# A hybrid encoder trunk: two projections moved up one place in the recurrent mixer, the last gates placed inside the output projection's first group, low parts issued ahead of recurrence steps

## The chip, the cores and the metric

The kernel runs on one core of a Trainium2 chip. The metric is the device time of one execution in microseconds, as a median of runs. A core has five engines that work side by side, each through its own instructions in order: PE (matmul), DVE (vector), ACT (scalar and lookup functions), POOL (general purpose) and SP (here it issues most DMAs). PE's weight loads are shown apart as PEld and overlap its matmuls.

## The reference, cut to what matters

Two layers over 1024 frames of width 1024, in float32. Layer 0 is a recurrent mixer and an MLP, layer 1 is chunked attention and an MLP. The change lies in layer 0's mixer and in the norms in front of the two MLPs.

```python
def recurrent_mixer(hn, w_in, conv_w, conv_b, gate_a_w, gate_a_b, gate_x_w, gate_x_b, lam, w_out):
    z = hn @ w_in
    gate, xr = jnp.split(z, 2, axis=-1)
    xr = causal_depthwise_conv(xr, conv_w, conv_b)
    y = rg_lru(xr, gate_a_w, gate_a_b, gate_x_w, gate_x_b, lam)
    return (y * jax.nn.gelu(gate)) @ w_out

def rg_lru(x, w_a, b_a, w_x, b_x, lam):
    ...
    r = jax.nn.sigmoid(jnp.einsum("bsnd,nde->bsne", xb, w_a).reshape(bsz, s, w) + b_a)
    i = jax.nn.sigmoid(jnp.einsum("bsnd,nde->bsne", xb, w_x).reshape(bsz, s, w) + b_x)
    log_a = (-LRU_C * r.astype(jnp.float32)) * jax.nn.softplus(-lam.astype(jnp.float32))
    a = jnp.exp(log_a)
    mult = jnp.sqrt(-jnp.expm1(2.0 * log_a))
    u = mult * (i * x).astype(jnp.float32)
    ...
    _, h = lax.associative_scan(combine, (a, u), axis=1)
```

The recurrence width is 1408: 11 tiles of 128 channels for the projections and the convolution, and 16 blocks of 88 channels for the gate weights. After the mixer comes `h = h + g1 * y`, then the second norm and a squared-ReLU MLP.

## The kernel before

**Arithmetic.** Everything lies transposed, channels on partitions and the 1024 frames in two halves of 512. Each float32 operand is split in a high part (a cast on ACT, line 196 for streamed data) and a low part (source minus high part, on DVE, line 200). A product is three matmuls of 512 columns: high by high, high by low, low by high (`mm3`, lines 329, 330 and 331).

**The stream.** Class `Stream` holds a list of items in the order in which they are loaded: weights, gate weights, modulation rows ("ada", used by one DVE operation at line 362 each), and rows of intermediate results that were put in DRAM. At most seven raw items lie in the chip at once; a later one is loaded by SP only when an earlier one is given back. Queue "w" turns weights into parts, queue "a" operands; `cap` bounds how many parts of each may be live. The casts are issued as soon as the caps allow; the low parts are put on a list (`los`) and are issued by `flush`.

**The tick.** The program order of the mixer is written out by hand. A call of `tick` stands after every few matmuls. It runs the jobs that are due (`at(d, f)` puts a job d ticks later: convolution copies, scans, products), then issues low parts up to a cost (`flush`; 2 in the mixer, where a low part of 512 columns costs 1 and one of 1024 costs 2), and then pumps the stream, which loads and casts. What is issued earlier stands earlier in each engine's queue.

**The mixer's steps.** `xr(t)` is the projection of channel tile t: 48 matmuls, two PSUM banks emptied by ACT (lines 916 and 918), then the convolution on DVE (line 923), copies from tiles to blocks by POOL's DMAs (line 931), and the split of the blocks (lines 937 on ACT and 944 on DVE). `gate(t)` is the gate projection of tile t: 48 matmuls, two banks, then a gelu on ACT (line 910). `recur(blocks)` does the gates of the blocks: per block 12 matmuls of 88 by 88 in four groups with one bank each, a sigmoid on ACT for each group (line 970), a product on DVE (line 975), then tanh, square root and exponential on ACT (lines 982, 987, 990, each with a table load between), and some ticks later the scan on DVE (lines 994 to 1001). Copies by POOL (line 1008) take the result back to tiles, where it is multiplied with the gelu (line 1014) and stored in DRAM as `ygd[t]`. `_done(t)` gives the blocks that are complete with tile t: two blocks for t = 2, 4, 6, 8 and 10, one for the others.

The order from tile 3 on was `xr(3)`, `recur` of blocks 0 and 1, `gate(2)`, `recur(_done(2))`, `gate(3)`, and then for t = 4 to 10 `xr(t)`, `recur(_done(t - 1))`, `gate(t)`. There are eight PSUM banks for all.

**The output projection** goes over four groups j of two output tiles. In each, part c = 0 takes the first three rows of `ygd` (36 matmuls in four chunks) and part c = 1 the next four (48 matmuls), into the same four banks, which DVE then adds into h (line 1097). `recur(_done(10))` stood after the first group. A last part (16 chunks of 12 matmuls) takes the remaining four rows; in its second half the norm `n2` begins: squares on ACT (line 541), adds of squares on DVE (line 542), a sum by matmul (line 550), a broadcast (line 566), scaling on DVE (line 605), shift and split on ACT (lines 610, 620) and low parts on DVE (line 623). The MLP follows at once. `NormS` is the class of `n2` and of the norm before the second MLP.

The parts after the first MLP and up to the second are ordered by a planner, not by hand.

Of the kernel before, what the change touches and what calls it, by code (L numbers as in the profile page):

```python
# [11 lines left out]
ALU = mybir.AluOpType  # L12
# [6 lines left out]
NT = 11  # L19
# [8 lines left out]
def _done(t):  # L28

    return [b for b in range(W // BLK) if (b * BLK + BLK - 1) // 128 == t]  # L30
# [35 lines left out]
class Stream:  # L66
# [8 lines left out]
    def __init__(self, nc, slot, wh, ws):  # L75
        self.nc, self.slot, self.wh, self.ws, self.ns = nc, slot, wh, ws, 7
        self.items = []
        self.loaded = self.raw = self.ring = self.pos = self.now = 0
        self.queue = {"p": [], "w": [], "a": [], "u": []}
        self.live = {"w": 0, "a": 0, "u": 0}  # L80
        self.cap = {"w": 8, "a": 0, "u": 3}

        self.lag = {"p": 4, "w": 0, "a": 2, "u": 4}
        self.hold = None
        self.used = -1

        self.stop = ()
        self.timed = self.early = False
        self.stored = set()
        self.los, self.jobs = [], []  # L90

# [212 lines left out]
def trunk(ctx: ExitStack, tc: tile.TileContext, I, out, dbg=None, stop=None):  # L304
# [87 lines left out]
    def some(n):  # L392
        for _ in range(n):
            if rest:
                ws.add(*rest.pop(0))
# [6 lines left out]
    def w_in(*us):  # L402
        for u in us:
            ws.add(I["w_in"][u], 1024)
# [1 line left out]

    w_in(NT, NT + 1, 0, NT + 2, 1, NT + 3)
    gate_item(_done(0) + _done(1))
    w_in(2)
    gate_item(_done(2))  # L410
    w_in(3)
    for t in range(4, NT):
        w_in(NT + t)
        some({8: 3, 9: 2, 10: 3}.get(t, 0))
        gate_item(_done(t - 1))
        w_in(t)
    gate_item(_done(NT - 1))
    ygd = dp.tile([NT, 128, S], F32, name="ygd")
    ygits = []
# [7 lines left out]
    def w_out(c, j):  # L427
        kn = 4 if c else 3
        ws.add(I["w_out"][c * 4 + j][:, : kn * 256], kn * 256)

    for j in range(4):
        if j == 0:
            yg_items(3)
        w_out(0, j)
        if j == 0:
            yg_items(4)
        w_out(1, j)
        some(4)
    yg_items(4)
    for j in range(4):  # L440
        w_out(2, j)

    rest = rest[:8] + part(1, 1) + part(1, 0)
    rest += ada_items(I["kvada"], kvmod, "kvb", 1, 8, 4, "kvg")
# [79 lines left out]
    class Norm:  # L524


        def __init__(self, h, a, sh):
            self.h, self.a, self.sh = h, a, sh
            self.acc = None
            self.r = slot()  # L530
            self.hh, self.hl = [None] * KD, [None] * KD

        def sq(self, k, cols, lag=1):
            n = cols.stop - cols.start
            if self.acc is None:
                self.acc = slot()
            if k == 0:
                A_.activation(out=self.acc[:, cols], in_=self.h[k][:, cols], func=AF.Square)
            else:
                t = slot()  # L540
                A_.activation(out=t[:, :n], in_=self.h[k][:, cols], func=AF.Square)
                ws.at(lag, lambda: V.tensor_tensor(out=self.acc[:, cols], in0=self.acc[:, cols],
                                                   in1=t[:, :n], op=ALU.add))

        def mm(self, half, ps=None):

# [40 lines left out]
    class NormS(Norm):  # L587
# [3 lines left out]

        def __init__(self, h, a, sh):
            super().__init__(h, a, sh)
            self.op = {}
            cnt[0] += 1
            self.dram = dp.tile([KD, 128, S], F32, name=f"hsp{cnt[0]}")

# [302 lines left out]
    at = ws.at  # L900

    def tick():
        ws.tick(2)

    xc, xb, yg, ym, xraw, R = {}, {}, {}, {}, {}, {}
# [112 lines left out]
    def recur(bs):  # L1018

        for b in bs:  # L1020
            gates(b)
        tanhs(bs)
        roots(bs)
        for n, b in enumerate(bs):
            at(3 + 2 * n, scan, b)
# [20 lines left out]
    def gate(t):  # L1046
        pss = []
        proj2(ws.next(), lambda half, ps: pss.append(ps))
        at(0, gelu, t, pss)
# [13 lines left out]
    xr(3)  # L1063
    recur(_done(0) + _done(1))
    gate(2)
    recur(_done(2))
    gate(3)
    for t in range(4, NT):
        if t == NT - 1:
            ws.cap["a"] = 6  # L1070
        xr(t)
        recur(_done(t - 1))
        if t == NT - 1:
            ws.cap["a"] = 14
        gate(t)
    h = []

    def load_h(n):
# [23 lines left out]
    for j in range(4):  # L1102
        if j == 2:
            ws.cap["a"] = 22
        its = [ws.next() for _ in range(2)]
        pss = [bank() for _ in chunks]
        for c, ys in enumerate((ygits[:3], ygits[3:7])):
            for ps, (half, e) in zip(pss, chunks):
                part_of(ps, its[c], e, half, ys, c == 0, c == 1)
                if c:  # L1110
                    into_h(2 * j + e, half, ps)
                elif j == 0 and half == 0:
                    load_h(2)
                tick()
            at(1, ws.done, its[c])
        if j == 0:
            recur(_done(NT - 1))
    ws.live["a"] -= 14
    ws.cap["a"] = 8
    its = [ws.next() for _ in range(4)]  # L1120
# [12 lines left out]
    for j in range(4):  # L1133
        for e in range(2):
            chunk(j, 1, e)
            n = 2 * j + e
            if n == 1:
                n2.mm(0)
            elif n == 3:
                n2.bc(0)  # L1140
            elif n > 3:
                n2.mod(0, (n - 4,))
            ws.tick()
        ws.done(its[j])
    ws.live["a"] -= 8
# [651 lines left out]
```

## Time and profile before

| what | value |
|---|---|
| median of 3 runs | 2348.17 us (2343.89 to 2348.65) |
| profiled execution | span 2341.0 us, first to last instruction; the page gives no other time of it |
| PE busy | 2255.9 us, 96% of the span |
| DVE, ACT, POOL busy | 75%, 53%, 17% of the span |
| mean granted TensorE clock | 0.989 |
| matmuls | 10588 |
| HBM read and written | 260.19 and 89.65 MB, 149 GB/s over the span |

A row of an instruction in the timeline has its start, its duration, the engine, the line of the kernel, the operation with its operands, and in brackets how long the engine stood idle before it and who ended that wait. Matmuls start about 0.23 us apart and each is shown as 0.39 us long, since they overlap; so the time that PE lost in a stretch is best read from the number of matmuls in it. The mixer and its output projection end at about 471 us of the span.

### The profile page before, as it was taken

Reading aid. Unit: us, or ns where it says so; the run is one execution under the profiler, and the core shown is the slowest. Engines: PE = TensorE matmul, PEld = TensorE weight load, DVE = VectorE, ACT = ScalarE, POOL = GpSimd, SP = SyncE. Lnnn points to the kernel's source line nnn. Section 1 sums busy time; section 2 is a strip of 40 time slices with the busy share of each in tenths; the row PEclk is TensorE's granted clock in tenths of the full one; section 3 lists DMA queues with packets and bytes.
Section 4 is the critical chain, followed back from the end, with each engine's and each line's share of the span. In section 5 each row is a group of like instructions: output and inputs, shape, how many; then the busy total and the mean of one; then the engine's idle time right before and its main releaser. Section 6 shows DMA issues by size and latency. Waiting matters only on the chain. (4 is left out here: it accounts for less than half of the span.)

```text
span 2341.0 us, 29502 instructions
## 1 busy us (share of the span) xinstructions
PE 2255.9 (96%) x10588; PEld 1872.1 (80%) x10588; DVE 1752.0 (75%) x2580; ACT 1245.2 (53%) x2148; POOL 394.9 (17%) x419
## 2 busy tenths in 40 slices
PE   4999989999999899999999999999999999899999
PEld 2878867878888788887888889998888888678887
DVE  8588887698787887777777639995495555877775
ACT  5597773375555633344443259994275555633342
POOL 0001010000000033330000248872000000033332
PEclk9999999999999999999999999999999999999999
DMA  8225456426676864445244200014114444854444
GB/s 317 72 78 147 132 192 223 178 76 238 243 257 243 315 227 150 154 160 194 101 143 133 88 10 11 10 60 147 65 59 167 172 171 176 301 205 156 149 146 142
DMA packets 141630, 363.31 MB, mean 155 GB/s; under 512 B 14924, under 2 KB 17100, under 8 KB 141484
## 3 DMA queue, kind: packets, MB, share of 16 engines
q1 hardware_dynamic: 113756, 278.45, 34.8%
q10 hardware_dynamic: 23824, 71.44, 8.3%
q0 software_dynamic: 3904, 11.54, 1.9%
q8 instruction: 83, 1.36, 0.2%
q14 instruction: 63, 0.52, 0.1%
HBM read 260.19 MB, written 89.65 MB: 149 GB/s over the span
## 5 line engine op out<-in xcount | busy, mean ns | idle before, releaser
L329 PE MATMUL b<-s,wh 128*128 128x512 f32 (+1 forms) x2532 | 999.0, 395 | 19.5 <-DVE s L1286 6.3
L330 PE MATMUL b<-s,wh 128*128 128x512 f32 (+1 forms) x2532 | 994.8, 393 | 16.9 <-DVE s L200 8.1
L331 PE MATMUL b<-s,wl 128*128 128x512 f32 x2296 | 903.0, 393 | 8.5 <-DVE wl L200 8.5
L329 PEld LDWEIGHTS b<-s,wh 128*128 128x128 f32 (+1 forms) x2532 | 478.2, 189 | 130.4 <-ACT wh L196 7.6
L330 PEld LDWEIGHTS b<-s,wh 128*128 128x128 f32 (+1 forms) x2532 | 478.3, 189 | 124.3 <-DVE s L200 9.7
L196 ACT ACTIVATE wh<-ws 128x1024 fp32r<-128x1024 f32 (+3 forms) x302 | 291.3, 975 | 477.4 <-POOL ws L126 277.0
L331 PEld LDWEIGHTS b<-s,wl 128*128 128x128 f32 x2296 | 433.6, 189 | 104.0 <-DVE wl L200 10.7
L200 DVE TENSOR_TENSOR wl<-ws,wh 128x1024 fp32r<-128x1024 f32 (+1 forms) x249 | 303.9, 1223 | 82.1 <-ACT wh L196 78.4
L1286 DVE SCALAR_TENSOR_TENSOR s<-b,mod,s 128x512 f32<-128x512 f32 x221 | 164.7, 746 | 113.8 <-PE b L331 113.6
L200 DVE TENSOR_TENSOR s<-ws,s 128x512 fp32r<-128x512 f32 x284 | 223.5, 802 | 5.9 <-ACT s L196 5.9
L126 POOL TENSOR_TENSOR ws<-ws 128x512 f32<-128x512 f32 x21 | 27.2, 1296 | 1109.3 <-DMA ws<-in_w_dram 671.3
L196 ACT ACTIVATE s<-ws 128x512 fp32r<-128x512 f32 x284 | 165.2, 618 | 77.6 <-DMA ws<-hid 37.4
L330 PE MATMUL b<-wl,s 128*128 128x512 f32 x384 | 149.9, 390 | 0.0
L329 PE MATMUL b<-wh,s 128*128 128x512 f32 x384 | 149.0, 389 | 0.0
L331 PE MATMUL b<-wh,s 128*128 128x512 f32 x384 | 146.5, 389 | 1.1 <-DVE s L584 1.1
L1264 DVE TENSOR_TENSOR s<-s,b 128x512 f32<-128x512 f32 x84 | 57.4, 684 | 112.8 <-PE b L331 96.4
L1262 ACT ACTIVATE s<-b 128x512 f32<-128x512 f32 x84 | 50.1, 596 | 100.7 <-PE b L331 100.7
L362 DVE CUSTOM_DVE_ANT_0 ws<-ws,cb,vec 128x1024 f32<-128x1024 f32 x59 | 75.0, 1279 | 32.2 <-DMA ws<-in_ada_dram 25.8
L331 PE MATMUL b<-s,wh 128*128 128x512 f32 x236 | 91.9, 389 | 0.0
L335 DVE TENSOR_TENSOR s<-b,s 128x384 fp32r<-128x384 f32 x144 | 82.7, 592 | 11.9 <-ACT s L334 11.3
L1578 POOL TENSOR_SCALAR s<-s,sm 128x640 f32<-128x640 f32 (+4 forms) x128 | 86.2, 685 | 22.3 <-DVE sm L1576 20.9
L1573 ACT ACTIVATE s<-s,sm 128x640 f32<-128x640 f32 (+4 forms) x128 | 88.3, 696 | 0.7 <-DVE sm L1571 0.7
(165 smaller groups left out, 2976.8 us busy)
## 6 DMA issues: line engine op xcount, KB each, us to landing
hid<-s ACTq DMA_DIRECT2D x128, 512.0 KB, 4.9
ws<-hid SPq DMA_DIRECT2D x118, 512.0 KB, 4.6
ws<-in_w_dram SPq DMA_DIRECT2D x220, 256.0 KB, 3.5
ws<-in_ada_dram SPq DMA_DIRECT2D x56, 512.0 KB, 4.5
s<-in_ada_dram SPq DMA_DIRECT2D x40, 512.0 KB, 7.4
ws<-in_w_in_dram SPq DMA_DIRECT2D x22, 512.0 KB, 7.8
hsp<-s SPq DMA_DIRECT2D x32, 256.0 KB, 2.0
s<-hsp SPq DMA_DIRECT2D x16, 512.0 KB, 6.8
```

The source lines that it names most:

```text
L196: self.nc.scalar.activation(out=hi[:rows, :n], in_=src, func=AF.Copy)
L200: self.nc.vector.tensor_tensor(out=lo[:rows, :n], in0=src, in1=hi[:rows, :n].bitcast(F32), op=ALU.subtract)
L329: PE.matmul(ps, ah, bh, start=start, stop=False, skip_group_check=more)
L330: PE.matmul(ps, ah, bl, start=False, stop=False, skip_group_check=more)
L331: return PE.matmul(ps, al, bh, start=False, stop=stop, skip_group_check=more).ins
L335: V.tensor_tensor(out=lo, in0=src, in1=hi.bitcast(F32), op=ALU.subtract)
L362: V.tensor_tensor_reduce(out=t, in0=t, in1=cb, op0=ALU.mult, op1=ALU.add, scale=1.0, scalar=bias, accum_out=dst)
L1262: A_.activation(out=t, in_=ps, func=AF.Copy)
L1264: V.tensor_tensor(out=t, in0=t, in1=ps, op=ALU.add)
L1286: V.scalar_tensor_tensor(out=t, in0=ps, scalar=g2[:, m : m + 1], in1=t, op0=ALU.mult, op1=ALU.add)
L1573: A_.activation(out=p[:, lo:640], in_=p[:, lo:640], func=AF.Exp, scale=-1.0, bias=m, accum_out=s1)
L1578: G.tensor_scalar(out=p[:, lo:640], in0=p[:, lo:640], scalar1=sm[:, 4 + e : 5 + e], scalar2=1.0, op0=ALU.mult, op1=ALU.mult)
```

## The change

Tile 4's projection `xr(4)` is put between `gate(2)` and `recur(_done(2))`, and `xr(10)` ahead of `gate(9)`; the stream's order follows. `recur(_done(10))` stands between parts c = 0 and c = 1 of the first output group. A flag `eager` lets each tick issue up to 8 units of low parts before the jobs that are due; it is on from `gate(10)` to the end of the first group, and the last part's second half gets such a flush as well. The second weight of the first group is loaded ahead of the four operands of part c = 1. Eight of the 16 modulation rows among the output weights are moved behind the last part's weights. In `NormS`, the adds of squares for k = 1 to 5 go from DVE to POOL. The x tiles that become h are loaded one per chunk in the first group, and `cap["a"]` is raised later.

```diff
@@ the stream's order
     w_in(NT, NT + 1, 0, NT + 2, 1, NT + 3)
     gate_item(_done(0) + _done(1))
-    w_in(2)
+    w_in(2, NT + 4)
     gate_item(_done(2))
     w_in(3)
-    for t in range(4, NT):
+    gate_item(_done(3))
+    w_in(4)
+    for t in range(5, NT - 1):
         w_in(NT + t)
-        some({8: 3, 9: 2, 10: 3}.get(t, 0))
+        some({8: 3, 9: 2}.get(t, 0))
         gate_item(_done(t - 1))
-        w_in(t)
+        if t < NT - 2:
+            w_in(t)
+    w_in(NT + NT - 1, NT - 2)
+    some(3)
+    gate_item(_done(NT - 2))
+    w_in(NT - 1)
...
         w_out(0, j)
+        w_out(1, j)
         if j == 0:
             yg_items(4)
-        w_out(1, j)
-        some(4)
+        some((0, 4, 4, 0)[j])
     yg_items(4)
     for j in range(4):
         w_out(2, j)
+        some((0, 4, 4, 0)[j])
@@ class Norm, sq (pool is 0; 6 in NormS)
-                ws.at(lag, lambda: V.tensor_tensor(out=self.acc[:, cols], in0=self.acc[:, cols],
-                                                   in1=t[:, :n], op=ALU.add))
+                eng = G if k < self.pool else V
+                ws.at(lag, lambda: eng.tensor_tensor(out=self.acc[:, cols], in0=self.acc[:, cols],
+                                                     in1=t[:, :n], op=ALU.add))
@@ the mixer's tick
     def tick():
+        if ws.eager:
+            ws.flush(8)
         ws.tick(2)
@@ the mixer's order
     xr(3)
     recur(_done(0) + _done(1))
     gate(2)
+    xr(4)
     recur(_done(2))
     gate(3)
-    for t in range(4, NT):
-        if t == NT - 1:
-            ws.cap["a"] = 6
+    recur(_done(3))
+    gate(4)
+    for t in range(5, NT - 1):
         xr(t)
         recur(_done(t - 1))
-        if t == NT - 1:
-            ws.cap["a"] = 14
-        gate(t)
+        if t < NT - 2:
+            gate(t)
+    xr(NT - 1)
+    gate(NT - 2)
+    ws.cap["a"] = 6
+    recur(_done(NT - 2))
+    ws.eager = True
+    gate(NT - 1)
+    ws.cap["a"] = 14
@@ the output projection's groups
                 if c:
                     into_h(2 * j + e, half, ps)
-                elif j == 0 and half == 0:
-                    load_h(2)
+                elif j == 0:
+                    load_h(1)
                 tick()
             at(1, ws.done, its[c])
-        if j == 0:
-            recur(_done(NT - 1))
+            if j == c == 0:
+                recur(_done(NT - 1))
+        ws.eager = False
@@ the last part, second half
                 n2.mod(0, (n - 4,))
+            ws.flush(8)
             ws.tick()
```

More of the change, by code (lines that the diff above doesn't have):

```diff
@@ L87, in __init__ @@
         self.stop = ()
-        self.timed = self.early = False
+        self.timed = self.early = self.eager = False
         self.stored = set()
@@ L528, in __init__ @@
             self.h, self.a, self.sh = h, a, sh
-            self.acc = None
+            self.acc, self.pool = None, 0
             self.r = slot()
@@ L593, in __init__ @@
             super().__init__(h, a, sh)
-            self.op = {}
+            self.op, self.pool = {}, 6
             cnt[0] += 1
```

## The prediction

> **What bounds the kernel now.** I read the page first: PE is busy 96% of the span, so only its idle time and its slow clock can be won. The span is all that the page gives of the profiled execution.
>
> ```profile
> span 2341.0 us, 29502 instructions
> ```
>
> Then I read the windows view, in stretches of 60 us over the part that the diff reorders (to about 480 us), with three short stretches behind. Columns: stretch, length, then busy time and instruction count of PE, PEld, DVE, ACT and POOL, granted clock, DMA share, GB/s.
>
> ```profile
> 180.00:240.00 60.00, 60.00 (x265) 48.28 (x264) 53.26 (x50) 46.29 (x56) 5.25 (x10) 1.00 0.49 146
> 120.00:180.00 60.00, 58.65 (x243) 45.90 (x242) 48.60 (x41) 51.49 (x59) 5.27 (x10) 0.94 0.30 88
> 300.00:360.00 60.00, 51.85 (x217) 41.22 (x217) 50.67 (x53) 40.86 (x52) 4.74 (x9) 0.91 0.65 215
> 420.00:480.00 60.00, 56.55 (x255) 46.23 (x254) 40.73 (x60) 23.65 (x35) 0.00 (x0) 1.00 0.39 143
> 138.00:144.00 6.00, 5.99 (x14) 4.00 (x14) 5.93 (x6) 5.99 (x10) 0.29 (x1) 0.50 0.00 1
> 345.00:351.00 6.00, 0.20 (x1) 0.20 (x2) 5.97 (x6) 0.00 (x0) 0.52 (x2) 0.58 1.02 414
> 478.00:480.00 2.00, 2.00 (x14) 1.73 (x13) 2.00 (x3) 0.00 (x0) 0.00 (x0) 1.00 0.00 1
> ```
>
> The first row is the clean rate: 60/265 = 0.2264 us a matmul. The second has 22 fewer: **S1, 5.0 us lost**. The third has 48 fewer: **S2, 10.9 us**. The fourth has 3.45 us of PE idle: **S3, 3.5 us**. Together 19.4 us, or 0.8%; nothing else in this part stops PE. Last I read who ended each wait. In the PE timeline:
>
> ```profile
> 137.19 0.47 PE L329 MATMUL b<-s,wh 88*88 88x512 f32 x1 [1.33 <-ACT s L910]
> ```
>
> S1 is a gate matmul of `recur(2)` that waits 1.33 us for a PSUM bank held by the gelu of `gate(2)`; then the clock stands at 0.50 for 6 us (row 138 to 144), so most of S1 is clock. The gelu was late because ACT had a chain ahead of it:
>
> ```profile
> 132.09 2.19 ACT L990 ACTIVATE s<-s,sp 88x1024 f32<-88x1024 f32 x2
> 134.19 1.04 ACT L937 ACTIVATE s<-s 88x1024 fp32r<-88x1024 f32 x1
> 135.25 1.28 ACT L910 ACT_TABLE_LOAD   x1
> 136.54 1.09 ACT L910 ACTIVATE s<-b 128x512 f32<-128x512 f32 x2
> ```
>
> S2, from PE's waits (total, times, longest) and the DVE timeline:
>
> ```profile
> PE b L330 <- DVE s L200: 8.1, 3, 6.0
> ```
>
> ```profile
> 343.15 1.28 DVE L200 TENSOR_TENSOR s<-ws,s 128x512 fp32r<-128x512 f32 x2
> 344.35 2.35 DVE L944 TENSOR_TENSOR s<-s,s 88x1024 fp32r<-88x1024 f32 x2
> 346.62 1.22 DVE L1000 TENSOR_TENSOR s<-s,s 88x1024 f32<-88x1024 f32 x1
> 347.87 2.29 DVE L1001 TENSOR_TENSOR_SCAN s<-s,s 88x1024 f32<-88x1024 f32 x1
> 350.08 1.26 DVE L200 TENSOR_TENSOR s<-ws,s 128x512 fp32r<-128x512 f32 x2
> 351.26 1.27 DVE L362 CUSTOM_DVE_ANT_0 ws<-ws,cb,vec 128x1024 f32<-128x1024 f32 x1
> 352.47 0.08 DVE L362 DVE_READ_ACCUMULATOR2_ANT mod<- 128x1 f32 x1
> 352.47 1.29 DVE L200 TENSOR_TENSOR s<-ws,s 128x512 fp32r<-128x512 f32 x2
> ```
>
> PE needs the low parts (L200) of four operands for part c=1 of the output projection's first group. They come two at a time, with recurrence work and a modulation row (L362) between. S3 is the same thing where the MLP begins:
>
> ```profile
> 475.26 1.41 DVE L542 TENSOR_TENSOR s<-s,s 128x512 f32<-128x512 f32 x2
> 476.58 1.29 DVE L623 TENSOR_TENSOR s<-s,s 128x512 fp32r<-128x512 f32 x2
> ```
>
> PE wants the first of these two L623 at about 473.7 and gets it at 477.2; adds of squares (L542) stand ahead of it. Here a gap of 3.45 us left the clock at 1.00 (row 478 to 480).
>
> **The change part by part.** No matmul is added or removed, so the sum is what becomes of S1, S2 and S3.
>
> *Tile 4 up one place.* `xr(4)`, 48 matmuls or 10.9 us, now stands between `gate(2)` and `recur(2)`. The stalled matmul was the 19th of `recur(2)`; it now comes 10.9 us later, at about 146.5, while the gelu is done at 137.6. What is late next: `recur(3)` follows `recur(2)` with only `gate(3)` between. Before, the gelu ended 17 us after its recurrence step's last matmul (120.6 to 137.6). By the same distance gelu(3) ends at about 165; with eight banks, its two are wanted again by `xr(5)` at 172.4. The cover is 7 us; if it went, each us late would cost one, and the clock. The one 512 KB weight load of the tile is one place up in SP's queue, its copies on POOL are up too; POOL is busy 5 of 60 us. **S1 goes whole: -5.0.**
>
> *Tile 10 up one place, last gates into the first group, low parts first.* I place PE from one row:
>
> ```profile
> 342.06 0.39 PE L329 MATMUL b<-s,wh 128*128 128x512 f32 x1
> ```
>
> This is the fifth matmul of c=1. Counted back at 0.2264: c=1 began at 341.2, c=0 (36 matmuls) at 333.0, `gate(10)` at 322.1. After, with S1 gone, all is 5.0 earlier: `xr(10)` 292.7, `gate(9)` 303.5, `recur(9)` 314.4, `gate(10)` 317.1, c=0 328.0, `recur(10)` 336.1, c=1 341.6. The operands of c=1 gain the 5.4 us of `recur(10)`. Against this, conv(10) on DVE now comes before the low parts of c=0:
>
> ```profile
> 311.66 1.22 DVE L944 TENSOR_TENSOR s<-s,s 88x1024 fp32r<-88x1024 f32 x1 [6.55 <-ACT s L937]
> ...
> 330.92 0.68 DVE L200 TENSOR_TENSOR s<-ws,s 128x512 fp32r<-128x512 f32 x1
> 331.52 2.59 DVE L923 SCALAR_TENSOR_TENSOR s<-s,vec,s 128x1023 f32<-128x1023 f32 x2
> ```
>
> DVE worked without a gap from 311.66, when ACT released it, to the last low part of c=0 at 331.6: 19.9 us. After, it starts at about 308.0 (5.0 earlier, but ACT first empties a bank of `xr(10)`, some 1.3 us) and has the convolution (three of 1.3, 3.9) inside, and the low part of the group's second weight, which is now loaded and cast ahead of four of the operands (1.2, twice the columns of an operand's 0.64): 333.0. The first chunk of c=0 wants its fifth low part at 329.6 and gets it at 332.4: **2.8 us late** where before had none. From there DVE took 22.2 us to the last low part of c=1 (331.6 to 353.8). After, the convolution (3.9), that weight's low part (1.2) and two modulation rows (2.7) are gone from this: 14.4, so the eighth is done at 347.4 and the seventh, which chunk 0 wants last, at 346.8.
>
> Then ACT. The four accumulators of the group hold four banks across `recur(10)`, whose eight gate groups share the other four: its fifth group needs the first sigmoid read.
>
> ```profile
> 335.01 1.05 ACT L196 ACTIVATE wh<-ws 128x1024 fp32r<-128x1024 f32 x1
> 335.96 4.27 ACT L196 ACTIVATE s<-ws 128x512 fp32r<-128x512 f32 x8
> 340.13 2.15 ACT L937 ACTIVATE s<-s 88x1024 fp32r<-88x1024 f32 x2
> 342.30 1.28 ACT L910 ACT_TABLE_LOAD   x1
> 343.59 1.09 ACT L910 ACTIVATE s<-b 128x512 f32<-128x512 f32 x2
> ```
>
> ```profile
> 364.21 5.55 ACT L970 ACTIVATE s<-b,vec 88x512 f32<-88x512 f32 x8 [2.63 <-PE b L331]
> ```
>
> Queued behind `gate(10)`: gelu with its table 2.4, eight casts 4.3, a weight cast 0.8, table load 1.3, first sigmoid 0.7 = 9.5 us. PE gets to the fifth group 48 matmuls, 10.9 us, after `gate(10)`, so ACT may be 1.4 us late there. ACT's chain from the gelu of `gate(9)` (at 314.4) on is, by these rows, gelu 1.1, table 1.3, four sigmoids 2.8, two casts 2.2, six casts 3.2, tanh, root and exponential at about 1.1 each (an estimate from the exponential's row) with two table loads, a weight cast 1.05: 17.5 us, to 331.9, 3.9 late at 328.0. So ACT alone would make PE lose 2.5 us by the fifth group; the 2.8 of c=0 cover that. c=1 starts at 344.4, and its seventh operand at 346.8, wanted after ten matmuls at 346.7, adds 0.1: **about 3 us of waiting**. The clock is unknown: 1.33 us idle dropped it in S1, 3.45 did not in S3. Ends 0 and 3.5 (S1's share), I take 2, near the middle. **S2 shrinks from 10.9 to 5.0: -5.9.** What is left of it has the ends 0 and the whole 10.9. On POOL's queue the copies of tile 10 now stand ahead of the copies of block 11's result and hold them until the convolution ends (about 316); these feed a product that DVE reaches only some 10 us later.
>
> The Trainium skill (TensorE: Matmul & The Clock Gate, Part 1) has the clock fall after an idle window of about 3.4 us. By that S2 would leave only its 3 us of waiting and the time would be 2333; the row of 138 to 144 speaks against it.
>
> *Eight modulation rows moved behind the last part's weights.* Loads of 512 KB and 1.36 us of DVE each, out of 338 to 368 and into about 400 to 440, where ACT and DMA have room. Nothing of the cost is on PE's path: the last weight behind them in SP's queue is wanted only six chunks (16 us) into the last part. If that cover failed, a late weight would cost some us of landing.
>
> *Adds on POOL, low parts flushed first (S3).* In the second half, the adds of k=1 to 5 leave DVE. DVE then reaches the last chunk about 1.0 us sooner (PE's own end bounds it), and the two adds of 475.26, 1.41 us, go behind the low part: it is done at about 474.8 instead of 477.2. **-2.3**, leaving 1.2. A POOL add is not on the path: chunks are 2.7 us apart and a POOL operation of this size takes 1.3 to 1.7 (below). The same edit in the last norm, before the second MLP, has no PE wait to win.
>
> ```profile
> L200 DVE TENSOR_TENSOR s<-ws,s 128x512 fp32r<-128x512 f32 x49 | 44.2, 901 | 0.0
> ```
>
> ```profile
> L126 POOL TENSOR_TENSOR ws<-ws 128x512 f32<-128x512 f32 x21 | 27.2, 1296 | 1109.3 <-DMA ws<-in_w_dram 671.3
> ```
>
> The first row is from 860 to 1000 us, where POOL adds tensors: the same L200 that takes 0.64 (350.08) takes 0.90 beside POOL. So each moved add may lengthen two DVE operations by 0.26: five adds, 2.6 us, against the 2.3 won. The Trainium skill (GPSIMD Engine Reference, Engine selection and Key points) says this too: two-input elementwise work belongs on VectorE, about 2x faster, and the two share SBUF interfaces.
>
> **Sum.** -5.0 - 5.9 - 2.3 = -13.2 on the profiled 2341.0, so 2327.8. The median of the runs lies 7.2 above that span: **2335**. The later stages have the same instructions; where they are ordered by a planner I allow 3 us either way.
>
> **The rivals.**
> 1. *All three go* (DVE and ACT catch up): 2348.2 - 19.4 = 2328.8. For: ACT's lateness is a sum of rough terms, and with 3 us less of it no wait is left. Against: DVE's lateness at c=0 has no such slack. Chance 0.20.
> 2. *S2 moves and keeps its size*: PE waits at c=0 and in `recur(10)` as long as it did at c=1, with the clock. For: DVE is at 5.97 of 6 (345 to 351). 2348.2 - 7.3 = 2340.9. Chance 0.14.
> 3. *POOL slows DVE*, S3 stays: 2337.5. Chance 0.08. Against: in 420 to 480 DVE is only 40.7 of 60 busy.
> 4. *The change doesn't do what it says*: S1 returns at a later recurrence step as ACT's chains stand closer, S2 keeps its size; only S3 shrinks: 2345.9. Chance 0.12.
> 5. *Slower*: `recur(10)` with four banks ties PE to ACT. Past 1.4 us each us of lateness costs one. Before, ACT began its gelu at 343.6, 10.6 us after `gate(10)`'s end; that lateness would cost 9.2 and the clock, about S2's own size. To undo all and lose 0.2% (4.7 us) takes 21 us of lateness, giving 2353. Chance 0.06.
>
> **How the numbers follow.** My forecast has 0.40, with its own range of 2331 to 2340. A measurement of this kernel tells about 0.2% from no change, 4.7 us, so below 2343.5 is faster: 0.40 + 0.20 + 0.14 + 0.08 = 0.82; within 0.12; slower 0.06. The range 2327 to 2346 takes in rivals 1 to 3 and half of 4.
>
> **What would show it.** Right: no PE wait and clock 1.00 from 115 to 165; PE waits of some 3 us in all at the start of c=0 on L200 and in the gates behind it on ACT's sigmoid; a wait of about 1 us on L623 where the MLP begins. Wrong: a wait on a gelu after `recur(3)`; a single wait over 4 us between 325 and 350; DVE operations longer than before at 430 to 475; a different PE idle share after 1100 us.

## The result, and the profile after

| what | before | after |
|---|---|---|
| median, runs on one chip | 2346.03 us (2342.2 to 2348.65) | 2332.78 us (2332.22 to 2335.35) |
| ratio after to before, 95% interval | | 0.9954 [0.9942, 0.9967] |
| profiled execution, span | 2341.0 us | 2330.4 us |
| mean granted TensorE clock | 0.989 | 0.994 |

Measured again on another chip beside the last experiment, the changed kernel's median was 2333.15 us at a ratio of 0.9956 [0.9942, 0.997]. The forecast was 2335 us, and 13.2 us less in the profiled execution; its span became 10.6 us shorter. The net is about right, but the three terms of the sum aren't, as the same stretches show. The windows view of the changed kernel, with columns as before (stretch, length, busy time and count of PE, PEld, DVE, ACT, POOL, then granted clock, DMA share, GB/s):

```profile
120.00:180.00 60.00, 57.48 (x246) 45.69 (x244) 43.87 (x38) 51.83 (x59) 4.72 (x9) 0.97 0.29 81
300.00:360.00 60.00, 58.51 (x253) 45.77 (x253) 50.28 (x51) 55.24 (x68) 4.74 (x9) 1.00 0.65 216
420.00:480.00 60.00, 57.57 (x256) 46.15 (x255) 37.24 (x57) 26.17 (x41) 13.65 (x10) 1.00 0.35 114
...
150.00:156.00 6.00, 5.67 (x18) 4.55 (x19) 5.93 (x6) 6.00 (x10) 2.60 (x5) 0.72 0.54 122
```

The first stretch had 243 matmuls before and has 246, 19 short of the clean 265: 4.3 us are still lost where 5.0 were. The second went from 217 to 253, a gain of 8.2 us. The third hardly moved, from 255 to 256. So S1 stayed, S2 gave more than forecast, and S3 gave little. PE's timeline of the changed kernel says which waits are left (in brackets the idle time and who ended it):

```profile
150.33 0.60 PE L329 MATMUL b<-s,wh 128*128 128x512 f32 x1 [2.52 <-ACT s L981]
333.67 0.50 PE L330 MATMUL b<-s,wh 128*128 128x512 f32 x1 [0.99 <-DVE s L200]
334.88 0.50 PE L330 MATMUL b<-s,wh 128*128 128x512 f32 x1 [0.24 <-DVE s L200]
336.08 0.50 PE L330 MATMUL b<-s,wh 128*128 128x512 f32 x1 [0.24 <-DVE s L200]
466.16 0.50 PE L330 MATMUL b<-s,wh 128*128 128x512 f32 x1 [1.64 <-DVE s L632]
468.51 1.05 PE L559 MATMUL b<-ones,s 128*128 128x1 f32 x8 [0.23 <-POOL s L551]
472.96 0.70 PE L575 MATMUL b<-s,ones 128*128 128x512 f32 x1 [0.55 <-DVE s L569]
```

(In the changed kernel the sigmoid is line 981, the gelu 921, the split's two halves 948 and 955, the norm's low part 632, its adds 551.) The gelu wait of `recur(2)` is gone, and a longer one has come at the first matmul of `gate(3)`, which wants a bank from the sigmoid; the short window above shows the clock at 0.72 behind it. ACT's and POOL's timelines of the changed kernel show what the sigmoid waited for:

```profile
140.46 0.60 ACT L929 ACTIVATE s<-b 128x512 f32<-128x512 f32 x1 [1.80 <-DVE s L1011]
148.30 1.28 ACT L981 ACT_TABLE_LOAD   x1 [4.75 <-DMA s<-s]
```

```profile
143.30 0.52 POOL L1019 DMA_DIRECT2D s<-s  x1 [22.03 <-ACT s L927]
```

A sigmoid doesn't read what a copy wrote. It waits for its *destination*: the kernel has 38 slots in on-chip memory for such results, and a slot comes back only when its last reader is done. The one copy under way was POOL's of block 0's result, issued at 143.30 and landed 4.9 us later, at 148.2. It was issued 0.55 us behind the end of the scan (142.75; the releaser in brackets is inferred, and another), and the scan stood behind the split of tile 3 on DVE:

```profile
134.95 1.22 DVE L955 TENSOR_TENSOR s<-s,s 88x1024 fp32r<-88x1024 f32 x1 [6.37 <-ACT s L948]
136.10 1.21 DVE L1005 SCALAR_TENSOR_TENSOR s<-s,s 88x1024 f32<-88x1024 f32 x1
140.46 2.29 DVE L1012 TENSOR_TENSOR_SCAN s<-s,s 88x1024 f32<-88x1024 f32 x1
```

DVE idles 6.37 us for ACT's half of that split, and only then begins the recurrence of block 0. Before the change this copy came at the same time (143.71); what is new is that a sigmoid with PE behind it asks for the slot.

To follow the offset between the kernels I took the start of the same matmul in both: 0.9 us at the gates of block 4 (163.84 before, 162.92 after), 9.65 at the start of the second output group (368.88 and 359.23), 9.98 at the norm's second broadcast (482.94 and 472.96), 10.6 at the end. So 8.7 of the 10.6 us lie in the 200 us between the first two points.

### The profile page after: what moved, and what is told of

Read it like the earlier page. It is cut to its first block, busy times and chain, and to the rows that moved or that the text cites. A ratio compares the mean times of both kernels' runs of the same rounds, so it can differ in the third digit from the quotient of the medians.

```text
span 2330.4 us, 29543 instructions
## 1 busy us (share of the span) xinstructions
PE 2248.5 (96%) x10588; PEld 1866.4 (80%) x10588; DVE 1742.8 (75%) x2560; ACT 1243.6 (53%) x2148; POOL 425.3 (18%) x439
## 5 line engine op out<-in xcount | busy, mean ns | idle before, releaser
L331 PEld LDWEIGHTS b<-s,wl 128*128 128x128 f32 x2296 | 432.5, 188 | 103.4 <-DVE wl L200 10.5
L335 DVE TENSOR_TENSOR s<-b,s 128x384 fp32r<-128x384 f32 x144 | 82.6, 593 | 11.1 <-ACT s L334 10.6
```

The source lines that it names most:

```text
L331: return PE.matmul(ps, al, bh, start=False, stop=stop, skip_group_check=more).ins
L335: V.tensor_tensor(out=lo, in0=src, in1=hi.bitcast(F32), op=ALU.subtract)
```

## The experiments

All are edits of the changed kernel, and "before" is the kernel before, run beside them on the same chip. Kernels run on different chips are compared by their ratios to it. The time to the norm's second broadcast matmul (472.96 in the changed kernel) is given beside the whole, since the later part differs from kernel to kernel by up to 3.7 us with the same waits; that comes last.

**1. Split of tile 3 six steps later.**

```diff
-        at(4 if late else 3, split_hi, t)
-        at(5 if late else 4, split_lo, t)
+        at(10 if t == 3 else 4 if late else 3, split_hi, t)
+        at(11 if t == 3 else 5 if late else 4, split_lo, t)
```

> What is read: the 192 matmuls from the gates of blocks 0 and 1 up to the gates of block 4. At the full rate they take 43.5 us; before took 48.8, after 48.2, with a wait of 2.5 us for a sigmoid at 150. Theory A (slots): that sigmoid waited for an SBUF slot, which a copy of block 0's result still held, because xr(4) moved up keeps two slots of its own. The split of tile 3's block, which is needed only two steps later, is put 6 ticks later here, so two slots are free at that place: the wait goes, the stretch takes 43.5 to 45.5, the whole kernel 2.5 to 4.5 us less than after (about 2329). Theory B (ACT's chains of two recurrence steps stand too close, whatever the slots): a wait of 1.5 us or more for ACT stays between 140 and 155, the stretch stays above 47, the time within 1 us of after.

Measured: 2330.8 us median, ratio 0.9948 [0.993, 0.9965]. The windows view of this kernel, columns as before, and PE's timeline:

```profile
120.00:180.00 60.00, 60.00 (x265) 48.28 (x264) 47.02 (x39) 54.55 (x64) 4.71 (x9) 1.00 0.28 82
300.00:360.00 60.00, 57.80 (x247) 45.55 (x246) 50.11 (x53) 53.48 (x66) 3.66 (x7) 0.97 0.67 231
```

```profile
329.93 0.50 PE L330 MATMUL b<-s,wh 128*128 128x512 f32 x1 [2.20 <-DVE s L200]
```

The first stretch runs at the clean 265 matmuls at full clock: the wait on the sigmoid is gone altogether, and the 192 matmuls take 43.8 us. The edit does two things. It asks for the split's slots later, and it takes the split out of the way of block 0's scan. POOL's and ACT's timelines of this kernel tell the two apart:

```profile
139.56 0.52 POOL L1019 DMA_DIRECT2D s<-s  x1 [18.91 <-issue]
```

```profile
142.95 1.28 ACT L981 ACT_TABLE_LOAD   x1
```

The copy behind that scan is 3.7 us earlier than in the changed kernel (0.6 of it POOL had won before), and lands 4.6 us after its issue, at 144.2. But the sigmoid's table load, which waited for it in the changed kernel, now begins at 142.95 without a wait, before the copy has landed. So this sigmoid no longer depends on that copy: it was given another slot. The earlier copy might have been enough by itself: in the changed kernel PE went on 2.0 us after that table load began, which from 144.2 would be 146.2, and PE comes there at 147.0 (an estimate). Either way the wait was for the slot, as theory A has it. Some 1.9 us of the gain come back at c=0, where PE now arrives earlier and waits 2.20 us instead of 1.47 in all, with some clock lost (247 matmuls, 0.97). The second broadcast comes at 469.57, 3.4 us earlier than in the changed kernel. On the whole time the gain of this run isn't clear of noise, since its interval overlaps with the changed kernel's.

**2. Tile 4 back in its old place** (its weights too).

```diff
-    xr(4)
     recur(_done(2))
     gate(3)
+    xr(4)
```

> Tile 4's projection is put back to its old place, all else as after. By the forecast's price of this edit (-5.0) the kernel would lose 4 to 5 us against after. By what the trace of after shows (the wait on the gelu replaced by a wait on a sigmoid, 48.8 against 48.2 us for the same matmuls) it loses 0.3 to 1 us: the wait of 1.3 us on the gelu of gate(2) is back with 6 us of half clock, and the 2.5 us wait on the sigmoid is gone.

Measured: 2339.05 us, one run. PE's timeline of this kernel:

```profile
136.97 0.73 PE L329 MATMUL b<-s,wh 88*88 88x512 f32 x1 [1.34 <-ACT s L921]
470.81 1.28 PE L559 MATMUL b<-ones,s 128*128 128x1 f32 x8 [1.35 <-POOL s L551]
```

The gelu wait is back at its old size. From the first gates to those of block 4 the kernel takes 48.5 us, 48.8 before the change and 48.2 after it. Moving tile 4 merely exchanged one wait for another. Its span is 6.9 us longer than the changed kernel's, and most of that comes from elsewhere: 1.2 us are behind by the norm's first row sum, 2.0 come in the norm, where GpSimd's sum is now 1.35 us late and the clock drops, and 3.7 after it, where nothing was edited.

**3. No early flush of the low parts.**

```diff
-    ws.eager = True
```

> The flag that puts low parts ahead of the due jobs is never set; all else as after. What is read: from the start of gate(10) to the end of the first output group, 156 matmuls, 35.3 us at full rate, 37.8 in after. Theory C (the order of the low parts is what shrank the second stall): the low parts come two per tick again with scans and splits between, c=0 or c=1 waits 3 us or more, the stretch takes 41 to 46 us. Theory D (the 5.4 us of gates between c=0 and c=1 shrank it, the order matters little): within 1.5 us of 37.8.

Measured: 2339.52 us, one run. PE's and DVE's timelines of this kernel:

```profile
338.50 0.79 PE L330 MATMUL b<-s,wh 128*128 128x512 f32 x1 [5.46 <-DVE s L200]
```

```profile
334.36 2.35 DVE L955 TENSOR_TENSOR s<-s,s 88x1024 fp32r<-88x1024 f32 x2
336.63 1.22 DVE L986 TENSOR_TENSOR s<-s,s 88x1024 f32<-88x1024 f32 x1
337.76 3.69 DVE L200 TENSOR_TENSOR s<-ws,s 128x512 fp32r<-128x512 f32 x6
```

The split of tile 10 and a recurrence product are ahead of the six low parts that c=0 needs, and one wait of 5.46 us takes the place of three that came to 1.47. The 84 matmuls of `gate(10)` and c=0 take 26.7 us instead of 21.4. So the order of the low parts is worth 5.3 us.

**4. Last gates behind the whole first group**, as before the change; the low parts stay early.

```diff
-            if j == c == 0:
-                recur(_done(NT - 1))
+        if j == 0:
+            recur(_done(NT - 1))
```

> The last gates stand behind the whole first group again, with low parts still issued first until then. Same stretch (156 matmuls, then with the gates last). Theory C (order of the low parts): no wait over 1 us at c=1, the stretch stays at 37 to 39. Theory D (the 5.4 us of gates): in after the low parts of c=1 are done between 347.2 and 351.4, and c=1 would begin at 342.8, so PE waits 3 to 5 us there and may lose up to 3.5 more to the clock: 41 to 46.

Measured: 2338.7 us, one run. PE's and DVE's timelines of this kernel:

```profile
346.85 0.50 PE L330 MATMUL b<-s,wh 128*128 128x512 f32 x1 [4.07 <-DVE s L200]
```

```profile
343.93 2.29 DVE L1012 TENSOR_TENSOR_SCAN s<-s,s 88x1024 f32<-88x1024 f32 x1
346.13 4.88 DVE L200 TENSOR_TENSOR s<-ws,s 128x512 fp32r<-128x512 f32 x8
```

c=0 waits as in the changed kernel, and then c=1 waits 4.07 us, since its low parts begin at 346.13 whatever PE does. From `gate(10)` to the end of the group, gates left out, it takes 38.7 us, and 32.3 in the changed kernel: 6.4 us. Theory C held in run 3 and theory D in run 4: the two edits remove waits at two different places, so S2 needed both.

**5. Sums of squares back on VectorE.**

```diff
-            self.op, self.pool = {}, 6
+            self.op, self.pool = {}, 0
```

> The six running sums of squares of each half that the change gave to GpSimd are VectorE's again (pool 6 becomes 0); all else is the changed kernel. Measure: from the first matmul of the second norm's row sums to the first matmul behind its second broadcast, 30.2 us before the change (453.24 to 483.40), 29.6 in the changed kernel (443.94 to 473.52), and the 128x1024 low part of VectorE within it, 1.2 us elsewhere and 2.31 beside GpSimd's sums. Theory E (GpSimd's sums are what eats the gain: they slow VectorE's operations and come late): the wait on GpSimd goes, VectorE's low part is back at 1.2 to 1.3 us, and the stretch takes 28.5 to 29.2. Theory F (moving the sums to GpSimd does help, little as it is): twelve sums of 0.68 us lie on VectorE again, of which some 2 to 4 us are in the way of the low parts, the wait of the first product on the low part grows from 1.64 to 2.5 or more, and the stretch takes 30.0 to 31. Behind the stretch nothing changes under either.

Measured: 2334.16 us median, ratio 0.9961 [0.9948, 0.9974], against 0.9954 with the sums on GpSimd. First the changed kernel's DVE and POOL timelines, then DVE's and PE's of this kernel:

```profile
455.89 2.31 DVE L200 TENSOR_TENSOR wl<-ws,wh 128x1024 fp32r<-128x1024 f32 x1
467.23 2.31 DVE L200 TENSOR_TENSOR wl<-ws,wh 128x1024 fp32r<-128x1024 f32 x1
```

```profile
455.69 1.43 POOL L551 TENSOR_TENSOR s<-s,s 128x512 f32<-128x512 f32 x1 [0.27 <-ACT s L549]
466.79 1.66 POOL L551 TENSOR_TENSOR s<-s,s 128x512 f32<-128x512 f32 x1 [9.67 <-DVE s L551]
```

```profile
467.33 1.22 DVE L200 TENSOR_TENSOR wl<-ws,wh 128x1024 fp32r<-128x1024 f32 x1
```

```profile
465.54 0.50 PE L330 MATMUL b<-s,wh 128*128 128x512 f32 x1 [2.17 <-DVE s L632]
```

The collision is real: a low part takes 2.31 us beside GpSimd's add and 1.22 without it. Both slow ones end 1.08 and 1.09 us after the add ends (457.12 and 468.45): as if DVE could only begin when GpSimd was through. This is what the Trainium skill says (SBUF — State Buffer, SBUF: two separate sides): the two share a pair of ports, and where a DVE operation has two inputs in SBUF and GpSimd's reads SBUF too, whichever begins first holds the pair for the whole instruction while the other is blocked. Yet neither theory's numbers came out. Without the adds on GpSimd the wait on the low part is 2.17 us instead of 1.64, and the smaller waits are gone, so the sums of the waits are 2.2 and 2.4 us: about the same. The stretch took 31.6 us and not 29.0 because the clock fell too, of which more below. The flag also sets where the adds of the norm before the second MLP run, here and in runs 8 and 10, so the parts behind the stretch aren't quite the same either.

**6. Modulation rows back among the output weights.**

```diff
-        some((0, 4, 4, 0)[j])
+        some(4)
     yg_items(4)
     for j in range(4):
         w_out(2, j)
-        some((0, 4, 4, 0)[j])
```

> Sixteen rows of the modulation are put back among the output projection's weights as before the change (four in each of the four places of the first part, none in the second); the rest is the changed kernel. Theory G (where these rows lie is of no account, since it is the low parts' and gates' order that shortened the first output group): the 84 matmuls of the last gate projection and the first part of the group take 21.4 us as in the changed kernel, within 0.5, the second part has no wait over 0.5, and the offset at the first broadcast of the norm moves by less than 1 us. Theory H (rows that are in VectorE's way there): the 84 matmuls and the rest of the first group grow by 2 us or more, by waits on the low part behind a row's reduction of some 1.2 us.

Measured: 2336.48 us, one run. The windows view of this kernel:

```profile
300.00:360.00 60.00, 58.51 (x254) 45.77 (x253) 50.52 (x53) 46.64 (x60) 4.74 (x9) 1.00 0.64 216
```

There are 254 matmuls where the changed kernel has 253; the 84 took 21.4 us, and the one new wait is 0.51 us at 379.82, past the first group. Where the rows lie is of no account for S2. This is theory G. The whole time is a single run, with later parts that weren't edited.

**7. Late split, and the second weight loaded behind the four operands again.**

```diff
         w_out(0, j)
-        w_out(1, j)
         if j == 0:
             yg_items(4)
+        w_out(1, j)
```

> Two edits on the changed kernel: the split of convolved tile 3 is made six steps later (as in the run of that edit alone), and the second part's weights of the output projection are loaded behind the four gated tiles again, so that their low part of 1.21 us no longer lies ahead of the six low parts that the first part waits for. Theory I (the first part waits for exactly what lies ahead of its low parts on VectorE): its wait goes from the 2.20 us of the late split alone to 1.0 to 1.2, the clock of that minute stretch is 1.00 again, the 84 matmuls take 21.0 to 22.0 instead of 23.3, and the second part has no wait over 0.5. Theory J (the weights' low part is then late for the second part instead): the second part waits 1 us or more, and what the first part gains is lost there. The time: 2328 to 2331 under I, 2330 to 2333 under J, with up to 3.7 us either way from the clock in later parts that the edit doesn't touch.

Measured: 2336.5 us median, ratio 0.9977 [0.9968, 0.9986]: worse than the changed kernel (0.9954 [0.9942, 0.9967]), and 3.5 us above theory J's 2330 to 2333, within the allowance for the clock. ACT's and PE's timelines of this kernel:

```profile
334.61 1.07 ACT L196 ACTIVATE wh<-ws 128x1024 fp32r<-128x1024 f32 x1 [2.30 <-DMA ws<-in_w_out_dram]
342.97 1.28 ACT L981 ACT_TABLE_LOAD   x1
```

```profile
345.01 0.73 PE L329 MATMUL b<-s,wh 88*88 88x512 f32 x1 [4.56 <-ACT s L981]
```

c=0 waits 0.93, 0.24 and 0.24 as theory I had it, but the weight's DMA is now late: ACT waits 2.30 us for it with the gelu, eight casts and the sigmoid behind, and the gates wait 4.56 us, with the clock at 0.59 and 0.56 in the two stretches of 6 us from 342 on. Theory J had the weight late, but for the second part; neither had the gates behind it. It is the tie of `recur(10)` to ACT that the prediction had as rival 5. Run 8 is this kernel with the sums on VectorE.

> The two edits of the run before, and the sums of squares on VectorE again (pool 0). Theory E: the stretch from the norm's first row sum to behind its second broadcast is shorter by 0.4 to 1.1 us than in the run before, and the time by as much. Theory F: longer by 0.4 to 1.5 us.

Measured: 2332.37 us median, ratio 0.9959 [0.9945, 0.9972]; from the norm's first row sum to its second broadcast 29.96 us, and 29.03 in run 7. The stretch is longer by 0.9 us, as theory F had it, but not for its reason: the waits sum to 2.2 us here and 2.4 in run 7, and the granted clock is 0.72 from 468 to 474, where run 7 has 1.00. On the whole time neither theory held: the median is 4 us lower than in run 7. Of this the two profiled executions show 2.5 us behind the norm (1856.4 us against 1858.9), where the flag moves adds too; the cause isn't shown.

**9. Late split, and operands' low parts ahead of the weight's.**

```diff
-        for low in self.los:
+        for low in sorted(self.los, key=lambda x: self.eager and x[1] > 1):
...
-    ws.cap["a"] = 6
+    ws.cap["a"], ws.eager = 6, True
     recur(_done(NT - 2))
-    ws.eager = True
```

> The split of convolved tile 3 six steps later, and in the early flush the gated tiles' low parts go ahead of a weight's: on VectorE the one low part of 1.21 us of the second part's weights moves behind the six of the gated tiles; ScalarE's and the queues' orders and the loads are those of the late split alone. Theory I (the first part waits for what lies ahead of its low parts on VectorE): the wait at the first part goes from 2.20 us to 0.9 to 1.1 (and two of 0.24), the clock is 1.00, the 84 matmuls take 21.2 to 22.0 us instead of 23.3, and the gates behind it wait for nothing, since ScalarE splits the weights where it did. Theory K (the gates behind the first part are bound by ScalarE as soon as the first part is on time, and the 4.56 us wait for the sigmoid comes back): the 24 matmuls of the gates take over 7 us instead of 5.5. Offset at the second broadcast under I: 467.9 to 468.6, and the time 2327 to 2331, or up to 3.7 more where the clock drops at a later gap.

Measured: 2329.37 us median, ratio 0.9935 [0.9923, 0.9947]. The windows view of this kernel and PE's timeline:

```profile
120.00:180.00 60.00, 60.00 (x265) 48.12 (x264) 46.32 (x40) 54.31 (x63) 4.73 (x9) 1.00 0.28 83
300.00:360.00 60.00, 58.60 (x253) 45.59 (x252) 49.95 (x53) 53.04 (x66) 3.67 (x7) 1.00 0.67 229
```

```profile
341.71 0.47 PE L329 MATMUL b<-s,wh 88*88 88x512 f32 x1 [0.86 <-ACT s L981]
```

Against run 1, one instruction moved on DVE up to the end of c=0 (a low part of 1.21 us). c=0 waits only 0.24 twice; the full clock is kept; and the gates wait 0.86 us on ACT, so there is a little of theory K in it. The second broadcast came at 469.20, 3.8 us earlier than in the changed kernel but 0.6 later than the latest that theory I gave, and only 0.4 earlier than in run 1: most of the gain is the late split's.

**10. The same with the flag `pool` at 4 instead of 6.** The first square of a half isn't an add, so this puts three adds of each half on GpSimd instead of five.

> The run before with four sums of squares of each half on GpSimd instead of six. Theory M (GpSimd's last sums are what collides with the 128x1024 low part of 2.31 us and comes 0.23 us late for the row sums): the wait on GpSimd goes, the second of the two slow low parts is back at 1.2 us, and from the norm's first row sum to the matmul behind its second broadcast it takes 28.0 to 28.9 us where the changed kernel took 29.0 (443.94 to 472.96). Theory N (what leaves GpSimd is in VectorE's way as before): the wait on the low part grows from 1.64 to 2 us or more and the stretch takes 29.1 to 30.5.

Measured: 2329.78 us median, ratio 0.9935 [0.9923, 0.9947]. The stretch took 29.2 us, with waits of 2.17 on the low part and 0.67 on the broadcast; GpSimd's 0.24 is gone. The 128x1024 low parts at those two places take 1.21 and 1.22 us, so the collision is gone too, and it bought nothing. Theory N, and no difference in time.

**11 and 12. The changed kernel and version 9 side by side on one chip**, both unaltered.

> The changed kernel itself, unaltered, beside the kernel before and the version of the next run on one chip. Theory O (what the profiles show of waits is what the clock on the wall shows): ratio to before 0.994 to 0.997 as the first time (0.9954), waits 2.4 to 2.6 us on the sigmoid near 150 us, 0.99, 0.24 and 0.24 at the first part of the first output group, 1.64, 0.23 and 0.55 in the norm. Theory P (the later parts differ from run to run by 3 to 4 us of clock and drown it): the same waits up to 500 us, but a span that is 2 us or more away from 2330.4.

> The version with the late split and the sorted low parts once more, on the same chip as the changed kernel of the run before. Theory O: 3.8 us were won up to the second broadcast of the norm (472.96 to 469.20), so its median is 2 to 5 us below the changed kernel's, and the ratio to before 0.993 to 0.995. Theory P: the medians lie within 2 us of each other.

Measured: 2333.15 us for the changed kernel (0.9956 [0.9942, 0.997]) and 2327.28 us for version 9 (0.9933 [0.9921, 0.9946]). Theory P fell, and theory O held with more than it asked: the changed kernel's waits repeat within 0.02 us, and version 9 is 5.9 us below it, where 2 to 5 were expected. Its slowest run (2330.51) lies under the changed kernel's fastest (2330.72), so it beats both kernels on this chip. The profiled executions show 3.2 of the 5.9 us, all up to the second broadcast (472.32 and 469.16); where the rest lies isn't shown. At c=0 version 9 waited 1.17, 0.24 and 0.24 us this time, where run 9 had no first wait.

## Why the prediction was right, and where it wasn't

- **"S1 goes whole: -5.0": wrong**, and the largest miss. The wait on the gelu went, as argued. The step that failed is "what is late next": it looked only at PSUM banks and found 7 us of cover there. Tile 4's own two destinations also take slots, ahead of the sigmoid's, and the sigmoid was then given a slot that block 0's copy still held. The new wait was 2.52 us with half clock behind it, so 0.7 us of the 5.0 were won (19 matmuls short instead of 22). Run 1 shows that the other 4.3 could be had by one split six steps later. Nearest in the prediction's list is rival 4's first half, but at the sigmoid instead of the gelu, and for slots instead of ACT's chains. ACT's timeline of before could have told it. A root (line 987) waits there for that same copy, and a sigmoid much later waits 4.30 us for another, which cost PE nothing:

```profile
149.02 1.06 ACT L987 ACTIVATE s<-s 88x1024 f32<-88x1024 f32 x1 [0.25 <-DMA s<-s]
325.54 1.28 ACT L970 ACT_TABLE_LOAD   x1 [4.30 <-DMA s<-s]
```

- **S2: mechanism right, size too small.** The forecast was 10.9 down to 5.0; 2.4 us were left (the 84 matmuls took 21.4 us, and at 0.2264 would take 19.0). DVE was placed well: PE began c=0 at 332.3, 4.3 us later than forecast, since S1 wasn't gone, and the fifth low part was done some 3.6 us later (332.94 and five times 0.61, in the row below, for 332.4). The terms that were mis-sized are the waiting, 1.47 us for about 3, and above all the clock: the 2 us allowed were not lost. Part of that is S1's doing. In run 1, where S1 is gone as the forecast assumed, the wait is 2.20 us, the clock 0.72 from 330 to 336, and 4.3 us are left of S2 (23.3 us for the 84 matmuls), near the forecast's 5.0. ACT's lateness in `recur(10)` didn't show here. The prediction had it covered by the wait at c=0; it showed at 0.86 us in run 9, where c=0 hardly waits, but also at 0.78 in run 12, where c=0 waits 1.65 in all, so that cover isn't all there is to it. The Trainium skill's rule on the clock (TensorE: Matmul & The Clock Gate, Part 1), by which the prediction gave 2333 us, agrees with S2, where no wait was over 0.99 us and the clock stayed at 1.00, and not with S1, where 2.52 us were enough. From DVE's timeline of the changed kernel:

```profile
332.94 3.69 DVE L200 TENSOR_TENSOR s<-ws,s 128x512 fp32r<-128x512 f32 x6
```

- **S3: "-2.3", measured -0.7** (29.70 us to 29.02 from the first row sum to the second broadcast). The wait went from 3.45 to 1.64, and not to 1.2, and two matmuls that hadn't waited now wait 0.23 and 0.55; the forecast put what comes behind the first wait at nothing. Run 5 parts it: without the adds on GpSimd the wait comes down from 3.45 to 2.17, and with them to 1.64. The 0.23 is GpSimd's. The 0.55 needn't be: it is there in run 10 too, at 0.67, where neither low part is slowed. By these waits the stretch would be 1.0 us shorter; why it is only 0.7 isn't shown. Rival 3's mechanism was real, but priced as 0.26 us on many operations, where it was 1.09 us on two of them; run 10, which is rid of them and no faster, speaks against it as the reason for the small gain.
- **The rows at no cost: right** for the first output group (run 6). The order of the other loads was varied only for the second weight (run 7), and there it mattered.
- **Later stages "3 us either way": about right.** From the second broadcast to the end it was 0.6 us here, and up to 3.7 in the runs above.

The net came out near by luck, because errors of both signs met. By the offsets above, the change won 0.9 us up to the gates of block 4, 8.7 from there to the second output group, 0.3 from there to the norm's second broadcast and 0.6 behind it. The forecast had 5.0, 5.9, 2.3 and nothing: 13.2 - 4.1 + 2.8 - 2.0 + 0.6 = 10.5, which is the measured 10.6 but for rounding. The step from span to median erred the other way: 7.2 us were added, as far as the median of before lay above the span of its one profiled execution, and the changed kernel's median lies 2.4 above its span. So 2.6 us too little was won, 4.8 too much was added, and 2332.78 came out 2.2 below the 2335. The medians themselves differ by 13.2 us on the first chip and by 9.8 on the last.

Of the prediction's signs, the first one for being right failed (the clock at 1.00 and no wait from 115 to 165), and one for being wrong came (DVE operations longer than before from 430 to 475). Run 1's kernel is the one that the forecast describes: its second broadcast comes 13.4 us earlier than before.

## What to carry to other kernels

When a step is moved up to cover a wait, check every resource that it takes earlier, and not only the one that was late: banks, and the on-chip slots too, where the trace shows a shortage as an engine waiting for a DMA that carries off something it never reads. Such waits are worth reading even where they cost nothing yet. Operands' low parts that PE wants next belong ahead of recurrence work: that order was worth 5.3 us in run 3. Putting them ahead of a weight wanted later as well cut the longest wait at c=0 from 2.20 us to 1.17 or none (runs 1, 12 and 9), of which 0.4 us was left at the norm. Adds taken from DVE to GpSimd won nothing that these runs show: with five, three and none of each half there, the waits in the norm came to 2.4, 2.8 and 2.2 us.

## What was not expected of the hardware

The length of a gap doesn't decide whether the clock falls. Runs 5 and 10 have the same wait of 2.17 us at the same matmul. The windows view of run 5:

```profile
462.00:468.00 6.00, 3.83 (x14) 2.77 (x13) 5.27 (x9) 3.34 (x5) 0.00 (x0) 0.86 0.41 131
468.00:474.00 6.00, 6.00 (x21) 5.05 (x20) 4.83 (x12) 1.45 (x3) 0.00 (x0) 0.57 0.25 87
```

The windows view of run 10, where the wait lies 2.4 us earlier:

```profile
462.00:468.00 6.00, 4.89 (x25) 4.20 (x26) 5.66 (x11) 2.22 (x5) 0.00 (x0) 1.00 0.41 131
468.00:474.00 6.00, 5.33 (x22) 3.62 (x21) 3.31 (x8) 4.11 (x8) 0.00 (x0) 1.00 0.35 129
```

Run 5 spends most of the following 6 us at half clock, and run 10 none. Run 8, with 2.17 us at that matmul once more, lies between (0.72 over 6 us). Before the change, a gap of 1.33 us cost 6 us at half clock and one of 3.45 us none. The Trainium skill (TensorE: Matmul & The Clock Gate, Part 1) has the clock fall after at least one idle window of about 3.4 us; what these traces show is falls behind gaps well under that, so as a length of gap the rule doesn't hold here. What else decides wasn't tried.

The granted clock differs between executions in later stages too. Windows of before, the changed kernel and version 9, one fence each:

```profile
1560.00:1620.00 60.00, 54.36 (x379) 50.28 (x379) 45.34 (x110) 43.48 (x100) 30.70 (x34) 0.94 0.37 126
```

```profile
1560.00:1620.00 60.00, 54.21 (x364) 48.60 (x363) 40.71 (x91) 38.03 (x83) 26.23 (x29) 1.00 0.40 141
```

```profile
1560.00:1620.00 60.00, 54.45 (x331) 48.19 (x330) 36.37 (x77) 33.92 (x72) 23.04 (x24) 0.94 0.40 145
```

The kernels are some 10 us apart here, so a stretch holds not quite the same matmuls, and their counts can't be compared. But PE's longest waits are the same in the first two, 2.5 us on ACT and 2.0 on DVE, and the clock is 0.94 and 1.00; 0.06 of 60 us is 3.6 us of full clock. In the changed kernel itself it was 1.00 in one profiled execution and 0.97 in the other. From the second broadcast to the end, where nothing was edited in runs 1 to 4, 7, 9, 11 and 12, their profiled executions took from 1856.5 us (run 9) to 1861.1 us (run 2). So two executions can lie some 4 us apart through the unedited part alone, which is more than several of the edits above are worth.
